# Block order at the end of an input projection, and scheduling priority for norms and last additions, in a hybrid encoder layer

## The chip, the cores and the metric

The kernel runs on one core of one Trainium2 chip. The metric is the device time of one execution in microseconds (us); lower is better. The engines are named as in the profile: PE (TensorE: matmuls, and PEld its weight loads), DVE (VectorE), ACT (ScalarE), POOL (GpSimd) and SP (SyncE, which here only issues DMA transfers; ACT issues some too).

## The reference

One encoder layer is applied to two groups of requests that share the weights: a prompt of 512 tokens and a sample of 1024, 1024 channels each. Shift, scale and gate come from a small product of each group's condition vector `c`. Cut to what matters:

```python
mod = (jax.nn.silu(c) @ w_ada + b_ada).reshape(b, N_MOD, 1, D_MODEL)
shift_a, scale_a, gate_a = mod[:, 0], mod[:, 1], mod[:, 2]
shift_m, scale_m, gate_m = mod[:, 3], mod[:, 4], mod[:, 5]

h = _rmsnorm(x, g_pre_mix) * (1.0 + scale_a) + shift_a
proj = h @ w_in                       # q 512 | k 128 | v 128 | u 512 columns
q = _apply_rope(_rmsnorm(q, g_q), cos, sin)
k = _apply_rope(_rmsnorm(k, g_k), cos, sin)
a = _attention(q, k, v)               # 8 query heads on 2 kv heads, bidirectional
p = _multiscale_pool(u, w_pool, pool_scale)
mix = jnp.concatenate([a, p], axis=-1) @ w_out
x = x + gate_a * _rmsnorm(mix, g_post_mix)

h = _rmsnorm(x, g_pre_mlp) * (1.0 + scale_m) + shift_m
f = jnp.square(jax.nn.relu(h @ w_ff1)) @ w_ff2
x = x + gate_m * _rmsnorm(f, g_post_mlp)
```

## The kernel before

Activations lie transposed, with channels on the 128 partitions and tokens along the free dimension, in stretches of 512 tokens: the prompt is one (c = 0, hf = 0), the sample two (c = 1, hf = 0 and 1). Most products are made from operands split into a rounded part and a remainder, three matmuls for each pair of 128x128 weights and 512 tokens (`block`, L156; `prod`, L869); ACT writes the rounded part, DVE the remainder (L139/L140, L881/L882, L743/L744).

The program is written as Python generators that `weave` (L25) interleaves: for each step of a foreground generator, a background generator is advanced by its rate. This fixes the order in which instructions are traced. A planner then orders them on each engine: each instruction has a priority, by default its place in the traced order, and whenever an engine is free in the planner's own model of time, the ready instruction with the earliest priority is issued next. The order so found is fixed in the program, and each engine works through its own in order. `tc.high_priority(n)` gives the instructions traced inside it the priority of a place n instructions earlier.

The order of the stages and the names that matter:

- `in_proj_p` (L488): the prompt's projection, L537 and L555.
- `in_proj_s` (L567): the sample's projection. The ten output blocks of 128 columns are taken in the order `S_IN` (L565): blocks 0 to 3 are queries, 4 keys, 5 values, 6 to 9 the pooling group's `u`. Each block has two stretches of tokens. The weights are loaded in the same order (`w_seq`). After its matmuls (L159 to L161) a query or key block is copied out of PSUM (`evac`, L377) and queued in `pend` for `qk_post` (L386): transposes on PE (`natural`, L383), squares, a sum (L395) and `rsqrt_small` (L165), the scaling and rotation on DVE (L400 to L410), transposes back, a split (L414, L415) and stores to `q_d`. `qk_post` is advanced one step at each step of the blocks that follow; what is left when the last block is done follows behind it. A pooling block is only copied and stored to `u_d` (L584); `u_post` takes it from there much later, beside the prompt's feed-forward.
- Woven into `in_proj_s` (L1302): `attention(0, ...)`, the prompt's attention (L591), at rate 1.2, and `gemv_cols` (L258) at rate 0.38: 24 of the modulation's products with `w_ada`, each a load of 512 KB on SP and one DVE instruction of 128x1024 elements (L236).
- Then `out_prep(0, 0)` (L719) loads and splits the output projection's operands, the pooled channels (k = 4 to 7) first, `out_proj(0, 0)` (L748) multiplies, with the sample's attention at rate 0.5 beside it, and `out_post(0, 0)` (L760) does the norm behind it, the gate, the residual and the next norm, with attention at rate 1.4.
- `ffn` (L825) is the prompt's feed-forward. The sample's output projection follows, and its feed-forward in a form with seven products for eight (`ff1_s`, L941; `ff2_s`, L1094).
- A norm over channels: `norm_vec` (L204) sums the squares over partitions by matmuls with one column of ones (`square_sums`, L194); `norm_sums` (L177) takes the reciprocal root of the means (ACT L170, L171; DVE L172 to L175), spreads it over the partitions by matmuls (L186) and copies the result (L191). `out_post` and `finish` call it.
- The last loop of `ff2_s` (L1213 to L1223) adds what is left of the second product to the accumulators in three parts: the first stretch of 512 tokens, then twice 256. For each of 8 blocks of channels: 12 matmuls, DVE's addition from PSUM (L1222), and `sumsq_last` (L813): ACT's square (L214), DVE's running sum (L216), and for the parts of 256 ACT's scaling by the gate (L821).
- `finish` (L1225), advanced one step at each step of that loop, does a part's norm, scaling (L1254 or L1245), residual (L1255 or L1246) and store (L1258). The part's last call runs behind everything else.

Of the kernel before, what the change touches and what calls it, by code (L numbers as in the profile page):

```python
# [7 lines left out]
F32 = mybir.dt.float32  # L8
# [3 lines left out]
AF = mybir.ActivationFunctionType  # L12
AL = mybir.AluOpType
# [3 lines left out]
KB = 8  # L17
NFB = 32
EPS = 1e-6

V_GPM, V_GQM, V_GPL, V_GQL, V_PS, V_B, V_C = 0, 8, 16, 24, 32, 36, 84
NV = 100
# [2 lines left out]
def weave(fg, bgs):  # L25

    credit = [0.0] * len(bgs)
    for _ in fg:
        for i, (bg, rate) in enumerate(bgs):
            credit[i] += rate  # L30
            while credit[i] >= 1.0:
                credit[i] -= 1.0
                next(bg, None)


def drain(g):
    for _ in g:
        pass


def chain(*gs):
    for g in gs:
        yield from g
# [3 lines left out]
def hymba_encoder_layer(ctx, tc, xp, xs, ns_, vec, gqk, rope, edge, ident_in, w_ada_c,  # L47
                        w_in_k, w_in, w_pool, w_out, w_ff1, w_ff2, yp, ys):
    nc = tc.nc
# [21 lines left out]
    st_p = ctx.enter_context(tc.tile_pool(name="stats", bufs=2))  # L71
    dram = ctx.enter_context(tc.tile_pool(name="dram", bufs=1, space=bass.MemoryType.DRAM))
    ps_mm = ctx.enter_context(tc.tile_pool(name="ps_mm", bufs=2, space=PSUM))
    ps_m = ctx.enter_context(tc.tile_pool(name="ps_m", bufs=1, space=PSUM))
# [24 lines left out]
    ident = const.tile([128, 128], F32, name="ident")  # L99
# [4 lines left out]
    eps_t = const.tile([128, 1], F32, name="eps_t")  # L104
    nc.vector.memset(eps_t, EPS)
    mod = const.tile([128, 48, 2], F32, name="mod")
# [40 lines left out]
    def next_w():  # L147

        while w_seq and len(w_ready) < AHEAD + 1:
            w_ready.append(load_w(*w_seq.pop(0)))  # L150
        return w_ready.pop(0)

    def mm_tile():
        return ps_mm.tile([128, 512], F32, tag="mm", name="mm")
# [10 lines left out]
    def rsqrt_small(out, m, n, shape, tag):  # L165

        ms = st_p.tile(shape, F32, tag=tag + "ms", name=tag + "ms")
        t = st_p.tile(shape, F32, tag=tag + "t", name="rs_t")
        u = st_p.tile(shape, F32, tag=tag + "u", name="rs_u")
        nc.scalar.activation(out=u, in_=m, func=AF.Ln, bias=eps_t, scale=1.0 / n)  # L170
        nc.scalar.activation(out=u, in_=u, func=AF.Exp, scale=-0.5)  # L171
        nc.vector.tensor_scalar(ms, m, 1.0 / n, EPS, op0=AL.mult, op1=AL.add)  # L172
        nc.vector.tensor_tensor(t, u, u, AL.mult)  # L173
        nc.vector.scalar_tensor_tensor(t, t, -0.5, ms, op0=AL.mult, op1=AL.mult)  # L174
        nc.vector.scalar_tensor_tensor(out, t, 1.5, u, op0=AL.add, op1=AL.mult)  # L175

    def norm_sums(m, keep=False):  # L177

        n = m.shape[1]
        rs = st_p.tile([128, n], F32, tag="nv_rs", name="nv_rs")
        rsqrt_small(rs, m, 1024.0, [128, n], "nv_")
        r = ps_m.tile([128, n * 128], F32, tag="m", name="nv_r")
        for j in range(n):
            nc.tensor.matmul(r[:, j * 128:(j + 1) * 128], lhsT=rs[:, j:j + 1].to_broadcast([128, 128]),  # L186
                             rhs=ident, start=True, stop=True)
        if keep:
            return r
        rt = st_p.tile([128, n * 128], F32, tag="nv_R", name="nv_R")  # L190
        nc.scalar.activation(out=rt, in_=r, func=AF.Copy)  # L191
        return rt

    def square_sums(m, sq, first, last):  # L194

        n = m.shape[1]
        for j in range(n):
            nc.tensor.matmul(m[:, j:j + 1], lhsT=sq[:, j * 128:(j + 1) * 128], rhs=ones[:, 0:1],  # L198
                             start=first and j == 0, stop=last and j == n - 1)

    def sums_tile(n=4):
        return ps_m.tile([128, 512], F32, tag="m", name="nv_m")[:, 0:n]

    def norm_vec(sqs, keep=False):  # L204

        m = sums_tile(sqs[0].shape[1] // 128)
        for i, sq in enumerate(sqs):
            square_sums(m, sq, i == 0, i == len(sqs) - 1)
        return norm_sums(m, keep)

    def sumsq_add(ss, src, m, eng):
# [350 lines left out]
            posts.append(qk_post(0, 0, xs_[b], b))  # L562
        rest.append(rp)

    S_IN = (4, 5, 9, 0, 8, 1, 7, 2, 6, 3)  # L565

    def in_proj_s():  # L567
        pend = []
        ws = {}
        for blk, hf in [(b, f) for f in range(2) for b in S_IN[:3]] + [(b, f) for b in S_IN[3:] for f in range(2)]:  # L570
            if hf == 0:
                ws[blk] = next_w()
            wh, wl = ws[blk]
            ps = mm_tile()
            for _ in block(ps, wh, wl, [h_t[1, hf, k] for k in range(KB)]):
                if pend and next(pend[0], 1) == 1:
                    pend.pop(0)
                yield
            if blk < 5:
                pend.append(qk_post(1, hf, evac(ps), blk))  # L580
            elif blk == 5:
                pend.append(v_post(1, hf, evac(ps)))
            else:
                put(u_d[blk - 6, :, hf * 512:(hf + 1) * 512], evac(ps))  # L584
        while pend:
            if next(pend[0], 1) == 1:
                pend.pop(0)
            yield
# [224 lines left out]
    def sumsq_last(c, hf, m, t0, n, fin):  # L813

        a = acc[c, hf][m][:, t0:t0 + n]
        if m == 0 and t0 == 0:
            ss_t[c, hf] = st_p.tile([128, 512], F32, tag="ss", name="ssf")
        ss = ss_t[c, hf][:, t0:t0 + n]
        sq = sumsq_add(ss, a, m, nc.vector)
        if n < 512:  # L820
            nc.scalar.activation(out=a, in_=a, func=AF.Copy, scale=gg_mlp[:, m, c:c + 1])  # L821
        if m == KB - 1:
            fin((c, hf, [ss, sq], t0, n))
# [270 lines left out]
    def ff2_s(pools):  # L1094
# [87 lines left out]
        for g, p, j in steps:  # L1182
# [15 lines left out]
            ps = chain_[j] if chained else mm_tile()  # L1198
# [14 lines left out]
        for hf, t0, n in ((0, 0, 512), (1, 0, 256), (1, 256, 256)):  # L1213
            for m in range(KB):
                if hf == 0 and 3 <= m + 2 < KB:
                    load_k(m + 2, pools["kp"])
                b = banks % 6
                banks += 1
                ps = (mm_tile() if b < 2 else ps_g.tile([128, 512], F32, tag=f"a{b - 2}", name="pb"))[:, :n]
                yield from prod(ps, wk[m], [tuple(x[:, t0:t0 + n] for x in fo["last", hf, k][0]) for k in range(4)])  # L1220
                a = acc[1, hf][m][:, t0:t0 + n]
                nc.vector.tensor_tensor(a, a, ps, AL.add)  # L1222
                sumsq_last(1, hf, m, t0, n, pools["fin"])  # L1223

    def finish(c, hf, sqs, t0=0, n=512, lands=4):  # L1225

# [55 lines left out]
    hs0, hs1 = hs[8:14] + hs[0:2], hs[2:8] + hs[14:16]  # L1282
    w_seq += [(w_in[b],) for b in S_IN]
    w_seq += [(w_out[m],) for m in range(KB)]
# [13 lines left out]
    bg = attention(0, att0)  # L1298
    gv = gemv_cols(0, cb0, 16, 40, inp)
    gv = chain([0] * 5, gv)  # L1300
    bg = chain([0] * 6, bg)
    weave(in_proj_s(), [(bg, 1.2), (gv, 0.38)])  # L1302
    drain(bg)
    drain(gv)
    att0_close()
# [17 lines left out]
    bg = attention(1, att1)  # L1323
# [17 lines left out]
    gv = gemv_rest()  # L1341
    fin = []
# [48 lines left out]
    pools = {}  # L1391
# [19 lines left out]
    fin = []  # L1411

    def close_w():
        for z in (wrb_close, wrx_close):
# [7 lines left out]
                 fin=lambda a: fin.append(finish(*a, lands=8)))  # L1422
# [79 lines left out]
```

## Time and profile before

| | us |
|---|---|
| median of 3 runs | 1666.7 (1665.64 to 1670.02) |
| the profiled execution | 1668.83 |
| its span, from the first to the last instruction | 1665.7 |
| DVE busy in it | 1213.7 |
| ACT busy in it | 854.8 |
| POOL busy in it | 10.4 |

The profiled execution is one more execution of the same program. The profile's timelines give for a row the start and the duration in us from the start of the span, the engine, the line, the operation, the tiles written and read, the shapes and a count of merged instructions; in brackets stands the idle time of the engine before it and what ended it. A row of several instructions is as long as all of them. The tile names in the rows are the program's: `nat` is a transposed block, `oh` and `ol` the parts of the output projection's operands, `q` in the last stage an accumulator, `x` a loaded residual, `ssf` the running sum of squares, `nv_m` and `nv_r` the norm's sums and its spread result.

### The profile page before, as it was taken

To read this page: it belongs to the slowest core of one execution; us is meant where nothing else is said; L and a number is where in the kernel's file an instruction comes from. 1 tells how busy PE (TensorE), PEld (TensorE's weight loads), DVE (VectorE), ACT (ScalarE), POOL (GpSimd) and SP (SyncE) were. 2 spreads that over 40 slices of the span, in tenths; PEclk is the share of its full clock that TensorE was granted. 3 is DMA by queue.
4 is the path that set the end of the run, shared out by engine and by line. 5 is a ranking of instruction groups with operands and counts; after the bars stand their busy time and mean duration, and the time that the engine had idled before them with its cause. 6 is when DMAs were issued, how large, how long until landed. Compare 5 with 4: busy or idle time off the path is not lost. (4 is left out here: it accounts for less than half of the span.)

```text
span 1665.7 us, 21550 instructions
## 1 busy us (share of the span) xinstructions
PE 1611.2 (97%) x7680; PEld 1299.9 (78%) x7680; DVE 1213.7 (73%) x1938; ACT 854.8 (51%) x1450; POOL 10.4 (1%) x27
## 2 busy tenths in 40 slices
PE   7999998999999999999999999899999999999996
PEld 4467886788888878888888888788888788888886
DVE  7898988568667675655667487878875576878757
ACT  2446664556645545546453475744445564444433
POOL 0000000000000000000000000000000000000002
PEclk8999999989999999999999999999999999999998
DMA  7756776443555553332368537566663745444334
GB/s 294 279 156 186 224 221 183 146 153 123 166 174 180 165 179 102 100 108 89 99 206 245 178 127 246 195 224 226 225 216 121 237 160 186 140 141 152 93 110 152
DMA packets 150618, 287.57 MB, mean 173 GB/s; under 512 B 15152, under 2 KB 56432, under 8 KB 150512
## 3 DMA queue, kind: packets, MB, share of 16 engines
q1 hardware_dynamic: 125824, 258.31, 47.9%
q10 hardware_dynamic: 24688, 27.89, 5.4%
q8 instruction: 60, 0.98, 0.2%
q14 instruction: 46, 0.38, 0.1%
HBM read 223.20 MB, written 61.37 MB: 171 GB/s over the span
## 5 line engine op out<-in xcount | busy, mean ns | idle before, releaser
L140 DVE TENSOR_TENSOR wl<-raw,wh 128x1024 fp32r<-128x1024 f32 (+2 forms) x106 | 121.1, 1142 | 70.4 <-ACT wh L139 69.9
L139 ACT ACTIVATE wh<-raw 128x1024 fp32r<-128x1024 f32 (+2 forms) x106 | 105.4, 995 | 120.4 <-PE mm L160 91.7
L630 ACT ACTIVATE p<-s,amx 128x1024 f32<-128x1024 f32 (+1 forms) x96 | 93.3, 972 | 108.6 <-DVE amx L628 106.7
L657 DVE TENSOR_TENSOR pl<-pT,ph 128x512 fp32r<-128x512 f32 x160 | 108.6, 686 | 54.8 <-ACT ph L656 54.3
L875 PE MATMUL pa<-fo,wh 128*128 128x512 f32 x448 | 140.4, 395 | 2.7 <-ACT x L1012 2.7
L628 DVE TENSOR_REDUCE amx<-s 128x1 f32<-128x1024 f32 (+1 forms) x96 | 100.1, 1042 | 43.5 <-PE s L618 43.1
L656 ACT ACTIVATE ph<-pT 128x512 fp32r<-128x512 f32 x160 | 93.4, 594 | 46.1 <-PE pT L653 36.8
L159 PE MATMUL mm<-hA,wh 128*128 128x512 f32 x256 | 106.7, 417 | 0.0
L159 PE MATMUL mm<-fh,wh 128*128 128x512 f32 x256 | 106.5, 417 | 0.0
L875 PE MATMUL mm<-fo,wh 128*128 128x512 f32 x336 | 104.8, 393 | 0.0
L875 PEld LDWEIGHTS pa<-fo,wh 128*128 128x128 f32 x448 | 84.8, 189 | 21.9 <-ACT x L1012 3.1
L161 PE MATMUL mm<-fh,wl 128*128 128x512 f32 x256 | 101.3, 396 | 0.0
L160 PE MATMUL mm<-fl,wh 128*128 128x512 f32 x256 | 101.0, 394 | 0.0
L160 PE MATMUL mm<-hA,wh 128*128 128x512 f32 x256 | 100.9, 395 | 0.0
L161 PE MATMUL mm<-hA,wl 128*128 128x512 f32 x256 | 100.5, 394 | 0.0
L653 PE MATMUL pT<-ident,p 128*128 128x128 f32 x640 | 96.6, 275 | 1.4 <-DVE pl L657 0.9
L618 PE MATMUL s<-kst,q 128*128 128x512 f32 x320 | 93.9, 406 | 4.0 <-ACT p L630 2.0
L653 PEld LDWEIGHTS pT<-ident,p 128*128 128x128 f32 x640 | 79.3, 142 | 22.6 <-issue 2.4
L875 PE MATMUL pa<-fo,wl 128*128 128x512 f32 x224 | 88.1, 393 | 0.0
L881 ACT ACTIVATE fo<-raw 128x512 fp32r<-128x512 f32 x106 | 66.3, 631 | 38.3 <-DMA raw<-f_d 31.5
L882 DVE TENSOR_TENSOR fo<-raw,fo 128x512 fp32r<-128x512 f32 x106 | 71.2, 689 | 15.8 <-ACT fo L881 15.2
L666 PE MATMUL x<-ph,vst 128*128 128x256 f32 x320 | 81.7, 285 | 0.5 <-ACT ph L656 0.5
(291 smaller groups left out, 3922.5 us busy)
## 6 DMA issues: line engine op xcount, KB each, us to landing
raw<-in_w_ff SPq DMA_DIRECT2D x56, 512.0 KB, 3.8
f_d<-x SPq DMA_DIRECT2D x98, 256.0 KB, 2.8
raw<-f_d SPq DMA_DIRECT2D x98, 256.0 KB, 3.0
raw<-in_w_ada_c SPq DMA_DIRECT2D x40, 512.0 KB, 3.9
g<-in_w_ada_c SPq DMA_DIRECT2D x24, 512.0 KB, 4.3
q<-q_d SPq DMA_DIRECT2D x96, 128.0 KB, 3.6
raw<-in_w_out SPq DMA_DIRECT2D x24, 512.0 KB, 3.8
rawx<-in_w_ff SPq DMA_DIRECT2D x20, 512.0 KB, 4.0
```

The source lines that it names most:

```text
L139: nc.scalar.activation(out=fh, in_=r[:, :n], func=AF.Copy)
L140: nc.vector.tensor_tensor(fl, r[:, :n], fh.bitcast(F32), AL.subtract)
L159: nc.tensor.matmul(ps, lhsT=wh[:, k, :], rhs=ah, start=(i == 0), stop=False)
L160: nc.tensor.matmul(ps, lhsT=wh[:, k, :], rhs=al, start=False, stop=False)
L161: nc.tensor.matmul(ps, lhsT=wl[:, k, :], rhs=ah, start=False, stop=(i == len(ks) - 1))
L618: nc.tensor.matmul(s[:, f * 512:(f + 1) * 512], lhsT=q[:, h, p, :], rhs=kst[c][:, kv, f * 512:(f + 1) * 512].bitcast(F32R), start=(p == 0) ...
L628: nc.vector.tensor_reduce(mx, s[:, :n], AX.X, AL.max, negate=True)
L630: nc.scalar.activation(out=pr, in_=s[:, :n], func=AF.Exp, bias=mx, accum_out=den)
L653: nc.tensor.transpose(t[:, k, :], pr[:, (4 * f + k) * 128:(4 * f + k + 1) * 128], ident)
L656: nc.scalar.activation(out=hi, in_=t, func=AF.Copy)
L657: nc.vector.tensor_tensor(lo, t, hi.bitcast(F32), AL.subtract)
L875: nc.tensor.matmul(ps, lhsT=x[:, k, :], rhs=y, start=start and k == i == 0, stop=k == n - 1 and i == 2, skip_group_check=not start)
```

## The change

Three things change. In `S_IN` blocks 7 and 2 change places, and 6 and 3, so that the projection ends with block 6 and not with block 3; the products of `w_ada` woven into it get rate 0.5 in place of 0.38. The norm's sums in `norm_vec` and the whole chain in `norm_sums` are traced with a priority 300 instructions earlier. The same holds for the addition and `sumsq_last` in the last loop of `ff2_s`. The sums of squares that `out_post` itself writes for the prompt's second norm keep their priority. What is computed stays the same.

```diff
+URGENT = 300

     def norm_sums(m, keep=False):
         n = m.shape[1]
-        rs = st_p.tile([128, n], F32, tag="nv_rs", name="nv_rs")
-        rsqrt_small(rs, m, 1024.0, [128, n], "nv_")
-        r = ps_m.tile([128, n * 128], F32, tag="m", name="nv_r")
-        for j in range(n):
-            nc.tensor.matmul(r[:, j * 128:(j + 1) * 128], lhsT=rs[:, j:j + 1].to_broadcast([128, 128]),
-                             rhs=ident, start=True, stop=True)
-        if keep:
-            return r
-        rt = st_p.tile([128, n * 128], F32, tag="nv_R", name="nv_R")
-        nc.scalar.activation(out=rt, in_=r, func=AF.Copy)
-        return rt
+        with tc.high_priority(URGENT):
+            rs = st_p.tile([128, n], F32, tag="nv_rs", name="nv_rs")
+            rsqrt_small(rs, m, 1024.0, [128, n], "nv_")
+            r = ps_m.tile([128, n * 128], F32, tag="m", name="nv_r")
+            for j in range(n):
+                nc.tensor.matmul(r[:, j * 128:(j + 1) * 128], lhsT=rs[:, j:j + 1].to_broadcast([128, 128]),
+                                 rhs=ident, start=True, stop=True)
+            if keep:
+                return r
+            rt = st_p.tile([128, n * 128], F32, tag="nv_R", name="nv_R")
+            nc.scalar.activation(out=rt, in_=r, func=AF.Copy)
+            return rt

     def norm_vec(sqs, keep=False):
-        m = sums_tile(sqs[0].shape[1] // 128)
-        for i, sq in enumerate(sqs):
-            square_sums(m, sq, i == 0, i == len(sqs) - 1)
+        with tc.high_priority(URGENT):
+            m = sums_tile(sqs[0].shape[1] // 128)
+            for i, sq in enumerate(sqs):
+                square_sums(m, sq, i == 0, i == len(sqs) - 1)
         return norm_sums(m, keep)

-    S_IN = (4, 5, 9, 0, 8, 1, 7, 2, 6, 3)
+    S_IN = (4, 5, 9, 0, 8, 1, 2, 7, 3, 6)

                 a = acc[1, hf][m][:, t0:t0 + n]
-                nc.vector.tensor_tensor(a, a, ps, AL.add)
-                sumsq_last(1, hf, m, t0, n, pools["fin"])
+                with tc.high_priority(URGENT):
+                    nc.vector.tensor_tensor(a, a, ps, AL.add)
+                    sumsq_last(1, hf, m, t0, n, pools["fin"])

-    weave(in_proj_s(), [(bg, 1.2), (gv, 0.38)])
+    weave(in_proj_s(), [(bg, 1.2), (gv, 0.5)])
```

## The prediction, made before the changed kernel ran

> **What bounds the kernel now.** I read the page first, then the list of PE's waits, then the timeline of each engine around the longest of them. The page says how much there is to win at all:
>
> ```profile
> PE 1611.2 (97%) x7680; PEld 1299.9 (78%) x7680; DVE 1213.7 (73%) x1938; ACT 854.8 (51%) x1450; POOL 10.4 (1%) x27
> ```
>
> PE is busy for 1611.2 of 1665.7 us. The change takes no matmul away, so it can win only PE's idle time, 54.5 us, and the time in which PE runs at a reduced clock. Both lie in few places. The first is the end of the input projection (PE's timeline):
>
> ```profile
> 273.91 0.40 PE L161 MATMUL mm<-hh,wl 128*128 128x512 f32 x1
> 275.86 0.66 PE L383 MATMUL nat<-ident,xT 128*128 128x128 f32 x4 [1.55 <-ACT xT L377]
> 276.38 0.74 PE L159 MATMUL mm<-oh,wh 128*128 128x512 f32 x2
> 281.90 1.08 PE L383 MATMUL nat<-ident,y 128*128 128x128 f32 x4 [4.79 <-DVE rs_t L173]
> 282.64 0.78 PE L160 MATMUL mm<-ol,wh 128*128 128x512 f32 x1
> ...
> 301.02 1.16 PE L618 MATMUL s<-kst,q 128*128 128x512 f32 x4 [1.79 <-DMA q<-q_d]
> ```
>
> The last projection matmul ends at 274.31. Then PE, which works in order, reaches the transposes (L383) of the last query block: it waits 1.55 us for the copy out of PSUM, does two matmuls of the output projection, and waits 4.79 us for the normed and rotated block. DVE shows what it waits for:
>
> ```profile
> 277.83 1.21 DVE L236 CUSTOM_DVE_ANT_0 g<-g,cb 128x1024 f32<-128x1024 f32 x1
> ...
> 281.07 0.68 DVE L410 TENSOR_TENSOR y<-y,t 128x512 f32<-128x512 f32 x1
> ...
> 281.75 0.68 DVE L744 TENSOR_TENSOR ol<-accA,oh 128x512 fp32r<-128x512 f32 x1
> ```
>
> The last instruction of the rotation (L410) ends at 281.75, and only behind it does DVE write `ol`, which the output projection needs. A modulation product (L236) of 1.21 us stands in the same stretch. The idle time has an after-effect, seen when stretches are cut at the clock's steps (columns: length, busy time of PE, PEld, DVE, ACT, POOL, then the granted clock, DMA share, GB/s):
>
> ```profile
> 175.00:200.00 25.00, 25.00 (x134) 20.13 (x134) 23.36 (x54) 16.49 (x37) 0.00 (x0) 1.00 0.68 205
> 200.00:225.00 25.00, 24.78 (x137) 20.45 (x136) 23.21 (x50) 15.65 (x35) 0.00 (x0) 1.00 0.76 231
> 225.00:250.00 25.00, 24.98 (x136) 20.52 (x135) 21.14 (x47) 15.18 (x33) 0.00 (x0) 1.00 0.73 235
> 279.84:286.67 6.83, 4.77 (x14) 3.93 (x15) 6.83 (x17) 1.52 (x4) 0.00 (x0) 0.50 0.14 29
> 358.35:372.00 13.65, 13.65 (x59) 12.66 (x59) 8.28 (x13) 6.29 (x11) 0.00 (x0) 0.50 0.52 188
> 1327.73:1331.14 3.41, 2.98 (x7) 2.40 (x8) 2.92 (x4) 2.02 (x4) 0.00 (x0) 0.50 0.99 300
> ```
>
> In 279.84 to 286.67 the granted clock is 0.50: the 4.77 us of PE work there would have taken half as long, so another 2.4 us are lost. The place costs 1.55 + 4.79 + 1.79 + 2.4 = **10.5 us**.
>
> The second place is the end (DVE's, PE's and ACT's timelines):
>
> ```profile
> 1646.31 2.48 DVE L1245 TENSOR_TENSOR q<-q,nv_r 128x512 f32<-128x512 f32 x4
> 1648.70 2.21 DVE L1246 TENSOR_TENSOR x<-q,x 128x512 f32<-128x512 f32 x2
> 1650.83 1.07 DVE L1222 TENSOR_TENSOR q<-q,pb 128x256 f32<-128x256 f32 x3
> 1651.83 0.94 DVE L216 TENSOR_TENSOR ssf<-ssf,sq 128x256 f32<-128x256 f32 x2
> ```
> ```profile
> 1646.03 3.57 PE L875 MATMUL pb<-fo,wk 128*128 128x256 f32 x28
> 1652.91 0.98 PE L198 MATMUL nv_m<-ones,ssf 128*128 128x1 f32 x4 [3.31 <-DVE ssf L216]
> 1653.76 0.99 PE L198 MATMUL nv_m<-ones,sq 128*128 128x1 f32 x4
> ```
> ```profile
> 1652.72 0.40 ACT L214 ACTIVATE sq<-q 128x256 f32<-128x256 f32 x1
> 1653.16 0.51 ACT L821 ACTIVATE q<-q,gg_mlp 128x256 f32<-128x256 f32 x1
> 1654.79 0.26 ACT L170 ACTIVATE rs_u<-nv_m,eps_t 128x2 f32<-128x2 f32 x1 [1.12 <-PE nv_m L198]
> ```
>
> The last product ends at 1649.60. Three additions (L1222) that PE's results have been ready for wait until 1650.83, because DVE first does the previous part's scaling and residual (L1245, L1246). From PE's end to the start of the last norm (L170) pass 5.19 us; everything behind is a serial chain to the last output.
>
> **Part 1: the block order and the faster modulation.** Block 3, a query block, gives the last place to block 6, a pooling block, which after its matmuls needs only a copy and a store. Block 3's two posts (the copy, two sets of transposes, the rotation, two stores each) then lie beside 48 matmuls of block 6 and no longer behind the projection. No instruction is added or removed; the order of the weight loads follows S_IN, and stores to u_d, read much later, merely change places on ACT's queue. So the 1.55 and 4.79 us go, and with them the reduced clock.
>
> The rate 0.5 for 0.38 draws the 24 products together:
>
> ```profile
> L236 DVE CUSTOM_DVE_ANT_0 g<-g,cb x24: 1201/1216/1226, 156.4 to 277.8; 128x1024 f32<-128x1024 f32 x24
> ```
>
> They stand (277.8 - 156.4) / 23 = 5.3 us apart; at the new rate 5.3 x 0.38 / 0.5 = 4.0 us. The last then comes about 23 x 1.3 = 30 us earlier, near 248, and the end of the projection is free of them. Their loads move with them on SP's queue, ahead of query and weight loads behind which they stood. The price is DVE in the middle: in 25 us there are 6.2 products instead of 4.7, 1.5 x 1.3 = 1.9 us more, where the rows leave it 1.64 and 1.79 us of idle time.
>
> What is late next? The output projection's own first operands. ACT's rows give 0.57 us for `oh`, DVE's row above 0.68 for `ol`:
>
> ```profile
> 275.22 0.58 ACT L377 ACTIVATE xT<-mm 128x512 f32<-128x512 f32 x1
> 275.70 1.14 ACT L743 ACTIVATE oh<-accA 128x512 fp32r<-128x512 f32 x2
> ```
>
> If they can be made only once the projection's tiles are free, PE waits 0.57 + 0.68 and two handovers, 1.5 us; if not, nothing. I take 1.5, since `oh` came only after 274.31 here too. The wait for `q` at 301.02 is for a load that is issued late because its buffer is freed late; with the posts gone it is issued earlier, but I don't see how early the planner puts the matmul: between 0 and 1.79, I take 0.9. For DVE's crowding I take 1.1, between 0 and 3.8 (1.9 us in each of two stretches). Sum: 10.5 - 1.5 - 0.9 - 1.1 = **7.0 us** won; at best 10.5, at worst 10.5 - 1.5 - 1.79 - 3.8 - 1.7 = 1.7.
>
> The last term, 1.7 us, is for the clock, from this row:
>
> ```profile
> 1328.16 1.22 PE L875 MATMUL pa<-fo,wh 128*128 128x512 f32 x2 [2.68 <-ACT x L1012]
> ```
>
> An idle time of 2.68 us was followed by 3.41 us at clock 0.50 (the last row of the stretches), which costs half of that. The Trainium skill, "TensorE: Matmul & The Clock Gate", section "HAM oscillation — how this bites in real kernels", asks for no idle gap above about 3.4 us. By that rule the remaining 1.5 us would never cost clock and the worst case would be 3.4; the trace does not agree, since 2.68 us were enough here.
>
> **Part 2: the additions.** With the higher priority L1222 and the squares behind it go ahead of L1245 and L1246 as soon as a bank is complete. After 1649.60 there remain one addition (1.07 / 3 = 0.36), its square (0.40), the last sums (0.99) and handovers (0.25): 2.0 us, and up to 1.1 more if DVE has just begun an L1246 (2.21 / 2). That is 2.0 to 3.1 instead of 5.19. I take a win of **2.5 us**. The displaced L1245 and L1246, 4.7 us, are not lost: DVE has nothing else to do while the last chain runs on PE and ACT. If that cover were gone, the last scaling would start up to 1.1 us late.
>
> **Part 3: the norms' chains.** The code runs eleven with sums of PE, and two more for the sample's first norm. In most of them PE has matmuls of another stage, so a shorter chain is worth nothing; where that cover is missing is the norm after the prompt's output projection, where PE has only attention:
>
> ```profile
> 348.04 0.16 DVE L173 TENSOR_TENSOR rs_t<-rs_u 128x4 f32<-128x4 f32 x1 [0.20 <-ACT rs_u L171]
> 348.12 1.22 DVE L628 TENSOR_REDUCE amx<-s 128x1 f32<-128x1024 f32 x1
> 349.25 0.15 DVE L174 SCALAR_TENSOR_TENSOR rs_t<-rs_t,nv_ms 128x4 f32<-128x4 f32 x1
> 349.32 0.68 DVE L657 TENSOR_TENSOR pl<-pT,ph 128x512 fp32r<-128x512 f32 x1
> 349.92 0.15 DVE L175 SCALAR_TENSOR_TENSOR nv_rs<-rs_t,rs_u 128x4 f32<-128x4 f32 x1
> ```
>
> A maximum and a subtraction of attention stand between the chain's instructions: 349.25 - 348.20 = 1.05 and 349.92 - 349.40 = 0.52 us, 1.6 in all. They move behind the chain, and attention is later by as much, beside matmuls that fill PE. I take **1.0 us**, between -1 (attention late) and 3.2 (twice 1.6, for the stage's second norm).
>
> **Sum.** 7.0 + 2.5 + 1.0 = 10.5 us. The profiled execution took 1668.83 us (span 1665.7), which gives 1658.3; the median of the runs is 1666.7, 2.1 less, which gives 1656.2. I predict 1656.2.
>
> **The rivals.** *Crowded DVE.* In 175 to 225 DVE has 3.4 us left, and the products want 3.8. If the posts and the prompt's attention fall behind by several us, the output projection waits for attention instead of for the post. Part 1 then wins about 1.7: 1666.7 - 1.7 - 2.5 = 1662.5. Against it: DVE's idle time before the end, and five products fewer there.
>
> *Full clock after the first output projection.* The 13.65 us at 0.50 cost 6.8 us. If shorter chains keep PE denser there, they come on top: 1656.2 - 6.8 = 1649.4. Against it: the sums' matmuls themselves, one column wide, fill much of that stretch.
>
> *The priority doesn't bite.* The planner orders each engine by readiness in its own model of time; if it believes L1222's input to be late, L1245 still goes first. Parts 2 and 3 win nothing: 1659.7.
>
> *Slower: PE's order.* An urgent matmul is put into PE's order where the model has its input ready; where DVE is later on the chip, everything behind it stands. The row for that:
>
> ```profile
> 1028.54 1.02 PE L198 MATMUL nv_m<-ones,ss 128*128 128x1 f32 x8 [0.78 <-DVE ss L216]
> ```
>
> 0.78 us here at the earlier priority. With two sums and one broadcast in eleven chains, 33 places: it eats the 10.5 us from 0.32 us a place on. At 0.78 each the cost is 25.7, the result 1666.7 - 10.5 + 25.7 = 1681.9; half of that gives 1669. For it speaks only that one row; against it that PE shows no wait at most of these matmuls.
>
> **How the numbers follow.** Forecast 0.56, with its own range 1651 to 1661; crowded DVE 0.14; full clock 0.12; no bite 0.12; PE's order 0.06. Within 0.3%, 5.0 us, a measurement of this kernel can't be told from no change: faster means below 1661.7, slower above 1671.7. Faster: 0.54 of the forecast, 0.12 of full clock, 0.10 of no bite, 0.02 of crowded DVE, 0.78. Slower: 0.04. The same: 0.18. For 8 in 10 the range takes in the crowded case above and most of the full clock's below: 1648 to 1665.
>
> **What would show it.** Right: between the last L161 of the projection and the second matmul of the output projection PE idles under 2.5 us, with no stretch at clock 0.50 behind; the last L236 stands before 260; L170 follows PE's last product within 3.2 us; no L628 or L657 stands inside L173 to L175. Wrong: PE waits for `ol` or `oh` of the attention heads, or for L383, for more than 3 us near 280; L1245 still ahead of L1222; new idle time before L198 or L186 elsewhere.

## The result, and the profile after

Five executions of each kernel, one beside the other on one chip: 1683.3 us (1676.89 to 1687.11) with the change, 1668.54 us (1665.64 to 1670.02) without it. The ratio is 1.0083 with an interval of [1.0059, 1.0108]: the changed kernel is **slower by 0.8%**, some 14 us, where 10.5 us less were predicted. In the changed kernel the lines behind the new `URGENT` have moved: up to 175 by one, the norm's broadcast from 186 to 188, its sums from 198 to 200, the lines of the posts, the attention and the output projection by three, those of the last additions by four.

The page's first part, for the profiled execution (span 1681.0 us, before 1665.7):

```profile
PE 1624.0 (97%) x7680; PEld 1310.0 (78%) x7680; DVE 1213.9 (72%) x1938; ACT 856.0 (51%) x1450; POOL 10.6 (1%) x27
```

The same 7680 matmuls keep PE busy for 1624.0 us in place of 1611.2. Of the 15.3 us that the span has grown, 12.8 are matmuls that take longer, and only 2.5 are idle time (1681.0 - 1624.0 = 57.0 against 54.5). In this profile the loss is mostly one of **clock**. Where it sits is seen when PE's first and last matmuls of each stage are set against each other:

| stage, by PE's matmuls, us | before | after | difference |
|---|---|---|---|
| start to the last matmul of the input projection | 274.31 | 267.45 | -6.9 |
| from there to the first of the prompt's output projection | 2.07 | 26.64 | +24.6 |
| the prompt's output projection | 65.85 | 59.69 | -6.2 |
| its post stage, to the first matmul of the feed-forward | 36.39 | 39.99 | +3.6 |
| from there to the last product of all | 1270.99 | 1273.68 | +2.7 |
| from there to the end | 16.10 | 13.59 | -2.5 |

The end is shorter by what was predicted. The projection ends 7 us earlier, and in the 26.6 us that follow PE is busy for only 12.9, most of them at half the clock. PE's timeline there:

```profile
267.06 0.39 PE L162 MATMUL mm<-hh,wl 128*128 128x512 f32 x1
268.24 0.73 PE L621 MATMUL s<-kst,q 128*128 128x512 f32 x2 [0.79 <-ACT p L633]
...
271.17 0.85 PE L656 MATMUL pT<-ident,p 128*128 128x128 f32 x4 [2.06 <-ACT p L637]
...
284.36 1.08 PE L386 MATMUL nat<-ident,y 128*128 128x128 f32 x4 [5.33 <-DVE y L413]
285.24 1.06 PE L656 MATMUL pT<-ident,p 128*128 128x128 f32 x4
...
294.09 0.79 PE L160 MATMUL mm<-oh,wh 128*128 128x512 f32 x1 [3.67 <-ACT oh L746]
```

Behind the projection stand the last units of the prompt's attention (`s`, `pT`) and the transposes of block 3's posts (`nat`), which the prediction had put beside block 6. For 5.33 us PE waits at a `nat` for the rotation, and the attention's `pT`, ready before, stands behind it in PE's order. The output projection then waits for `oh`. ACT's timeline shows why that comes so late:

```profile
267.40 0.69 ACT L633 ACTIVATE p<-s,amx 128x512 f32<-128x512 f32 x1 [3.09 <-DMA q<-q_d]
...
285.48 0.60 ACT L417 ACTIVATE rh<-nat 128x512 fp32r<-128x512 f32 x1 [4.58 <-PE nat L386]
...
289.60 0.38 ACT L674 ACTIVATE ao<-x 128x256 f32<-128x256 f32 x1 [2.68 <-PE x L670]
290.46 0.60 ACT L417 ACTIVATE rh<-nat 128x512 fp32r<-128x512 f32 x1 [0.47 <-PE nat L386]
290.46 0.38 ACTq L675 DMA_DIRECT2D a_d<-ao  x1
291.81 1.25 ACTq L422 DMA_DIRECT2D q_d<-rh  x2
293.40 2.19 ACT L746 ACTIVATE oh<-accA 128x512 fp32r<-128x512 f32 x4 [2.35 <-issue]
```

`oh` stands behind the attention's last copy (`ao`, 289.60), the last post's copy (`rh`, 290.46) and its stores (291.81). Before, it stood ahead of both last posts. ACT's timeline of the kernel before, where `oh` came at 275.70:

```profile
283.02 0.60 ACT L414 ACTIVATE rh<-nat 128x512 fp32r<-128x512 f32 x1 [1.67 <-PE nat L383]
...
290.29 0.60 ACT L414 ACTIVATE rh<-nat 128x512 fp32r<-128x512 f32 x1 [6.67 <-PE nat L383]
```

The last post is copied at 290.29 before and at 290.46 after: the work beside the matmuls ends at the same moment in both. Before, its last part lay beside the output projection; now that waits for all of it. Two stretches at half the clock lie in this gap, a third stands later, in the post stage (columns as in the prediction):

```profile
271.57:274.98 3.41, 3.41 (x16) 2.95 (x14) 1.83 (x4) 1.68 (x5) 0.00 (x0) 0.51 0.24 87
281.73:298.80 17.07, 9.94 (x30) 7.59 (x31) 11.85 (x23) 5.93 (x11) 0.00 (x0) 0.50 0.43 117
370.48:390.96 20.48, 20.48 (x95) 19.99 (x95) 12.28 (x21) 8.43 (x16) 0.00 (x0) 0.50 0.42 142
```

The first two are new or longer (before, 6.83 us in all); the third was 13.65 us long, and another 3.41 us are new ahead of it, from 360.24.

The end, on PE, ACT and DVE:

```profile
1663.50 3.93 PE L878 MATMUL pb<-fo,wk 128*128 128x256 f32 x31
1669.39 0.58 PE L200 MATMUL nv_m<-ones,ssf 128*128 128x1 f32 x4 [1.96 <-DVE q L1249]
```
```profile
1670.45 0.26 ACT L171 ACTIVATE rs_u<-nv_m,eps_t 128x2 f32<-128x2 f32 x1 [1.41 <-PE nv_m L200]
```
```profile
1667.64 0.41 DVE L1226 TENSOR_TENSOR q<-q,pb 128x256 f32<-128x256 f32 x1
1667.97 0.68 DVE L1250 TENSOR_TENSOR x<-q,x 128x512 f32<-128x512 f32 x1
1668.57 0.67 DVE L1249 TENSOR_TENSOR q<-q,nv_r 128x512 f32<-128x512 f32 x1
```

The addition now follows 0.21 us behind the last product (1667.43), and the norm begins 3.02 us behind it in place of 5.19.

### The profile page after: what moved, and what is told of

Its sections match the earlier page's. It is cut to its first block, busy times and chain, and to the rows that moved or that the text cites. A ratio compares the mean times of both kernels' runs of the same rounds, so it can differ in the third digit from the quotient of the medians.

```text
span 1681.0 us, 21539 instructions
## 1 busy us (share of the span) xinstructions
PE 1624.0 (97%) x7680; PEld 1310.0 (78%) x7680; DVE 1213.9 (72%) x1938; ACT 856.0 (51%) x1450; POOL 10.6 (1%) x27
## 4 chain that ended last, share of the span: by engine, by line
PE 79%; DMA 10%; DVE 7%; ACT 2%; issue 2%; SPq 1%; DVEq 0%; ACTq 0%
PE pa L878 19%; PE mm L160 9%; PE mm L161 9%; PE mm L162 9%; PE mm L878 9%; DMA raw<-in_w_ada_c 5%; PE pc L878 5%; PE s L621 3%; PE pT L656 3%; PE nv_m L200 2%; PE x L670 2%; PE x L669 2%; PE pb L878 1%; DVE raw L239 1%; DMA raw<-in_w_ff 1%
## 5 line engine op out<-in xcount | busy, mean ns | idle before, releaser
L660 DVE TENSOR_TENSOR pl<-pT,ph 128x512 fp32r<-128x512 f32 x160 | 108.8, 686 | 60.2 <-ACT ph L659 60.0
L631 DVE TENSOR_REDUCE amx<-s 128x1 f32<-128x1024 f32 (+1 forms) x96 | 100.0, 1041 | 41.1 <-PE s L621 40.7
L670 PE MATMUL x<-pl,vst 128*128 128x256 f32 x320 | 83.4, 291 | 0.5 <-DVE pl L660 0.3
```

Source lines behind the costliest of these rows:

```text
L631: nc.vector.tensor_reduce(mx, s[:, :n], AX.X, AL.max, negate=True)
L660: nc.vector.tensor_tensor(lo, t, hi.bitcast(F32), AL.subtract)
L670: nc.tensor.matmul(x, lhsT=v, rhs=st["pl"][:, k], start=False, stop=(k == nkb - 1))
```

## The experiments

Each is an edit of the kernel before unless it says otherwise. Ratios are against the kernel before on the same chip; the time in us is the ratio's, at 1670. Two theories stood at first for the projection, **R** (the higher rate crowds DVE) and **O** (the order itself), and **N** for the norms' priority.

**1 to 4: the parts of the change alone and in pairs.** Order alone, rate alone, both priorities without them, and order with rate:

```diff
e1  -S_IN = (4, 5, 9, 0, 8, 1, 7, 2, 6, 3)    +S_IN = (4, 5, 9, 0, 8, 1, 2, 7, 3, 6)
e2  -[(bg, 1.2), (gv, 0.38)]                  +[(bg, 1.2), (gv, 0.5)]
e3  the changed kernel with S_IN and the rate of before
e4  e1 and e2
```

> Only the order of the blocks is changed (block 6 last), against the kernel before. Theory R (the rate is to blame: the faster products crowd DVE, so that the posts and the prompt's attention fall behind): without the rate this order behaves as was forecast, the stretch from the last projection matmul to the first output-projection matmul stays under 6 us, and the time is 5 to 9 us below the kernel before. Theory O (the order is to blame: with a pooling block last the projection's matmuls run ahead, and attention's last units and the last post are left with nothing beside them): that stretch is 15 to 27 us here too, and the time is 5 to 12 us above.

> Only the rate of the modulation's products is changed (0.5 for 0.38). Theory R: attention falls behind, the projection's last matmul comes earlier than at 274.3 and the gap behind it grows from 2 us to over 10; the time is 5 to 12 us above the kernel before. Theory O: nothing is late at the end, DVE is freer there, the 4.79 us wait shrinks; the time is 0 to 4 us below.

> Both priorities are changed, the order and the rate are those of before. If the loss lies in the projection alone (theories R and O): the projection's end is as before (last matmul near 274, output projection from 276), the tail behind the last product is 2 to 3 us shorter, and the time is 1 to 4 us below. Theory N (the norms' priority in the sample's first norm or the prompt's second shifts the stages behind it): the stretch from the output projection's end to the first feed-forward matmul grows from 36.4 to 39 us or more, as in the changed kernel (40.0), and the time is the same or above.

> Order and rate are changed, the priorities are not: the changed kernel without parts 2 and 3. If the parts add up, this is the changed kernel less the tail's gain: the gap behind the projection 20 to 27 us, the stretch between output projection and feed-forward 36.4 us, and the time 8 to 14 us above the kernel before. If the gap comes only with the norms' priority (theory N, through the sample's first norm), the gap is under 6 us and the time below.

| kernel | ratio, interval | us | attention's last copy | projection's last matmul | gap behind it | output projection's last matmul |
|---|---|---|---|---|---|---|
| before | | | 271.2 | 274.3 | 2.1 | 342.2 |
| e1 order | 1.0018 [1.0003, 1.0032] | +3.0 | 283.0 | 273.3 | 16.0 | 347.0 |
| e2 rate | 1.0015 [0.9998, 1.0032] | +2.5 | 277.9 | 269.3 | 10.6 | 344.5 |
| e4 order and rate | 1.0059 [1.0038, 1.0081] | +9.9 | 289.0 | 265.7 | 27.8 | 351.7 |
| after | 1.0083 [1.0059, 1.0108] | +13.9 | 289.6 | 267.5 | 26.6 | 353.8 |
| e3 priorities | 1.0039 [1.0024, 1.0054] | +6.5 | 271.2 | 274.2 | 2.5 | 342.8 |

Neither R nor O is the cause alone. The attention's last copy is the last start in these rows (the line of `ao`, one row from each of before, e1, e2, e4 and after):

```profile
L671 ACT ACTIVATE ao<-x x16: 363/386/398, 150.9 to 271.2; 128x256 f32<-128x256 f32 x16
```
```profile
L671 ACT ACTIVATE ao<-x x16: 367/386/395, 151.3 to 283.0; 128x256 f32<-128x256 f32 x16
```
```profile
L671 ACT ACTIVATE ao<-x x16: 364/386/394, 151.0 to 277.9; 128x256 f32<-128x256 f32 x16
```
```profile
L671 ACT ACTIVATE ao<-x x16: 380/384/396, 149.5 to 289.0; 128x256 f32<-128x256 f32 x16
```
```profile
L674 ACT ACTIVATE ao<-x x16: 373/384/393, 150.4 to 289.6; 128x256 f32<-128x256 f32 x16
```

The order delays it by 11.8 us, the rate by 6.7; together that is 18.5, and e4 shows 17.8, the changed kernel 18.4. **The delays of the attention add up.** The times may not (3.0 and 2.5 alone, 9.9 together), but the 4.4 us between sum and pair are within what the three intervals allow. In each row the earlier end of the projection and the shorter output projection together give back more than half of what the gap has grown by; the output projection ends 4.8, 2.3 and 9.5 us later. In e3 attention and gap are as before: the norms have no part in it, and their price lies elsewhere.

**5: is it the attention's end?** New order and rate, and the attention woven in faster (theory G), against rival D, that DVE's work decides, whoever has it first:

```diff
 (with the new S_IN)
-weave(in_proj_s(), [(bg, 1.2), (gv, 0.38)])
+weave(in_proj_s(), [(bg, 1.6), (gv, 0.5)])
```

> New order and new rate, and the prompt's attention woven at 1.6 instead of 1.2 steps. Theory G (the output projection cannot start before the attention's last unit is stored and its operands stand behind the last units and posts in ScalarE's order, so the attention's end is what the gap of 27.8 us waits for): attention's last copy at 268 to 276 us instead of 289, the gap 8 to 16 us, 5 to 12 us faster than the kernel with order and rate alone. Rival D (VectorE's work up to that point decides, whoever gets it first): what the attention wins the posts lose, and the start of the output projection or its first stretch moves by under 3 us.

The time falls to 1.0002 [0.9987, 1.0017], 9.5 us under e4. The row of `ao` and the output projection's first row on PE:

```profile
L671 ACT ACTIVATE ao<-x x16: 373/384/412, 150.1 to 265.2; 128x256 f32<-128x256 f32 x16
```
```profile
278.28 0.74 PE L159 MATMUL mm<-oh,wh 128*128 128x512 f32 x2 [1.30 <-ACT oh L743]
```

The attention ends 24 us earlier than in e4 and the gap is 1.3 us. G holds. But the projection's matmuls end at 277.0, and the output projection at 342.2, where it ended in the kernel before: with all in its place the new order wins nothing.

**6 and 7: is it DVE's load?** New order and rate with DVE relieved, by GpSimd, or by halving the products (e11 leaves out the second half of each product's columns, so its output is not the layer's; it measures and is no kernel to use):

```diff
e10 +                if jb % 2:
    +                    nc.gpsimd.tensor_tensor(r, r, cb, AL.mult)
    +                    nc.scalar.activation(out=r, in_=r, func=AF.Copy, accum_out=mod[:, jb, c:c + 1])
    +                else:
                         tc.keep_in_program_order(gemv_part(c, jb, r, cb, r))
e11 -                tc.keep_in_program_order(gemv_part(c, jb, r, cb, r))
    +                tc.keep_in_program_order(gemv_part(c, jb, r[:, :512], cb[:, :512], r[:, :512]))
```

> New order and new rate, and every second product of the modulation (12 of 24, 1.2 us of VectorE each) made by GpSimd with ScalarE's sum. Theory D (VectorE's load decides when the attention and the posts end): 12 x 1.3 = 15.6 us less VectorE work ahead of the gap; attention's last copy 8 to 15 us earlier than 289 us, gap 12 to 20 instead of 27.8 us, 6 to 12 us faster than the kernel with order and rate alone. Rival (in-order waits on ScalarE and TensorE set it, not the load): gap over 24 us, time within 3 us of that kernel.

> New order and new rate, and each of the 24 modulation products woven into the projection is made over the first half of its columns only, so the modulation from column 16 on is not the reference's. Takes 24 x about 0.6 = 14 us from VectorE ahead of the gap and leaves the rest of the program as it is. Theory D (VectorE's load decides when the prompt's attention and the posts end): attention's last copy 8 to 14 us earlier than in the kernel with order and rate alone, where the gap was 27.8 us; gap 10 to 20 us, output projection over 7 to 13 us earlier, 6 to 12 us faster in all. Rival Q (the attention's place in the weave and the in-order waits decide, not the load): gap over 23 us, time within 3 us of that kernel.

e10 missed altogether: 1.0157 [1.0132, 1.0182], 26 us slower than the kernel before, the projection's last matmul at 295.2. It took nothing from DVE. One product on POOL, and DVE's row beside it:

```profile
185.77 2.35 POOL L270 TENSOR_TENSOR g<-g,cb 128x1024 f32<-128x1024 f32 x1 [6.84 <-DMA g<-in_w_ada_c]
```
```profile
185.83 2.57 DVE L640 TENSOR_SCALAR p<-p,aden 128x512 f32<-128x512 f32 x1
```

This scaling has a median of 0.486 us in the kernel before; here it takes 2.57 us and ends where POOL's product has ended. DVE's busy time is 1215.5 us with 12 products fewer. So e10 says nothing on D. e11 does: 0.9988 [0.9970, 1.0006], 12 us under e4, with 12.9 us less on DVE (busy for 1200.9 us, in e4 for 1213.8):

```profile
L671 ACT ACTIVATE ao<-x x16: 375/386/393, 150.2 to 277.1; 128x256 f32<-128x256 f32 x16
```
```profile
282.31 0.79 PE L159 MATMUL mm<-oh,wh 128*128 128x512 f32 x1 [4.11 <-ACT oh L743]
```

The attention ends 12 us earlier than in e4, the gap is 4.8 us, and the output projection ends at 341.6, 10 us earlier than in e4. Both are true, then: the attention's end sets the gap, and DVE's load, or the attention's share of DVE, sets the attention's end. Rival Q falls.

**8 to 11: where do the norms lose?** All norms alone; then without the priority in the prompt's post stage; then in the sample's post stages alone; then outside the post stages alone:

```diff
e6  the priority in norm_vec and norm_sums, nothing else of the change
e12 +with tc.high_priority(pr):      pr = URGENT, but 0 in out_post(0, 0)
e14 +with tc.high_priority(pr) if pr else nullcontext():      pr = URGENT in out_post(1, ...) alone
e15 the same, pr = URGENT in all but out_post
```

> Kernel before with the norms' priority alone. Theory N (it costs in the two stages behind the prompt's output projection, where the kernel with both priorities was 2.3 and 3.5 us longer, and the last additions' part gives back 2.5 there): 7 to 9 us slower, with about 20 us at a granted clock of 0.50 behind the prompt's output projection, and an end as long as before. Rival: the loss of the kernel with both priorities came from their sum: then 3 us slower or less.

> The norms' priority alone, but not in the post stage of the prompt's output projection. Theory N1 (the loss of 7 us sits in that stage, where attention's work that filled PE is used up early and PE is left with one-column matmuls at half the clock): the stage is 36 to 37 us again, with at most 14 us at half the clock, and the whole is within 2.5 us of the kernel before. Rival N2 (the loss is spread over the later stages, in half-clock stretches of their own): the stage is back and 4 to 5 us of the loss remain.

> The norms' priority in the sample's post stages alone, everything else as before. Theory S (the second half's post stage, where in the last run the first broadcast came 6 us sooner, but the additions behind it waited for their inputs' DMAs, VectorE had put the weights' splits off, and PE stood 2.5 us and fell to half the clock for 7 to 10 us): nearly the whole loss, 4 to 7 us slower; first broadcast 4 us behind the last output-projection matmul instead of 9.6, PE's wait for the second norm about 2.5 instead of 0.4 to 0.8 us. Rival T (the loss is in the norms outside the post stages): within 1.5 us of before.

> The norms' priority outside the post stages alone (the two inputs' norms and the final ones). Theory S: within 1.5 us of before. Rival T: 4 to 7 us slower, to be seen at the start of the program or in the last part, whose last matmul was 0.6 us later with the priority.

| kernel | ratio, interval | us | prompt's post stage | end of the sample's output projection to the next stage's first product (`pc`) |
|---|---|---|---|---|
| before | | | 36.4 | 79.5 |
| e6 | 1.0041 [1.0021, 1.0061] | +6.8 | 38.7 | 83.9 |
| e12 | 1.0040 [1.0024, 1.0057] | +6.7 | 36.4 | 83.3 |
| e14 | 1.0017 [1.0002, 1.0033] | +2.8 | 36.5 | 84.5 |
| e15 | 0.9995 [0.9983, 1.0008] | -0.8 | 36.5 | 79.5 |

The norms' price as a whole is clear, 6.8 us by e6, and e15 has none of it. Where it is paid inside the post stages is less clear: these two stages are compared by one profile each, and what such a profile is worth is said at each. In the prompt's post stage the chain itself is no shorter; DVE's timeline of the changed kernel:

```profile
359.92 0.15 DVE L174 TENSOR_TENSOR rs_t<-rs_u 128x4 f32<-128x4 f32 x1
359.99 0.68 DVE L660 TENSOR_TENSOR pl<-pT,ph 128x512 fp32r<-128x512 f32 x1
360.59 0.15 DVE L175 SCALAR_TENSOR_TENSOR rs_t<-rs_t,nv_ms 128x4 f32<-128x4 f32 x1
360.66 0.68 DVE L660 TENSOR_TENSOR pl<-pT,ph 128x512 fp32r<-128x512 f32 x1
361.26 0.15 DVE L176 SCALAR_TENSOR_TENSOR nv_rs<-rs_t,rs_u 128x4 f32<-128x4 f32 x1
```

Subtractions of the attention (L660) still stand between its steps, as each step waits for the one before and other work fits between; `nv_rs` is done 7.6 us behind the output projection (353.78), before 7.8. What moved is PE's order behind it. PE's timeline of e6, then its window at half the clock:

```profile
354.28 4.33 PE L200 MATMUL nv_m<-ones,x 128*128 128x1 f32 x24 [0.82 <-ACT x L780]
```
```profile
355.36:375.84 20.48, 20.48 (x94) 19.99 (x94) 12.28 (x21) 8.32 (x16) 0.00 (x0) 0.50 0.46 143
```

The stage is at half the clock for 20.48 us, before for 13.65, although PE is busy all the time; in e12 and e14, with no higher priority there, the stage is back at 36.4 and 36.5 us. That the new order is the reason is **not shown**. The 24 one-column matmuls in a row are no news (before, 32 follow one another from 355.14 on). And e8 has PE's matmuls of this stage in the very order of the kernel before, and yet this window:

```profile
357.86:378.34 20.48, 20.48 (x91) 19.37 (x91) 12.12 (x20) 9.12 (x18) 0.00 (x0) 0.50 0.44 145
```

Its stage is 39.0 us long. The twelve other profiles in this document that keep that order have 35.7 to 37.8 us, the three with the new one (after, e3, e6) 40.0, 38.7 and 38.7. So the 2.3 us are likely, but one profile in thirteen shows them without the priority.

The other place is the post stage of the sample's second half. PE's timeline of e14 there, where the output projection ends at 1002.69, and the kernel before's first broadcast, where it ended at 1000.68 (its sums behind are in the prediction, at 1028.54):

```profile
1006.37 1.13 PE L189 MATMUL nv_r<-ident,nv_rs 128*128 128x128 f32 x8
1030.06 1.02 PE L201 MATMUL nv_m<-ones,ss 128*128 128x1 f32 x8 [2.81 <-DVE ss L220]
```
```profile
1010.29 1.13 PE L186 MATMUL nv_r<-ident,nv_rs 128*128 128x128 f32 x8
```

The first broadcast comes 3.7 us behind the output projection in place of 9.6: here the priority shortens what it was meant to shorten. But the second norm's sums start 27.4 us behind it, before 27.9, so of 5.9 us only 0.5 are left at the stage's other end. DVE's timeline of e14 between them shows the new wait:

```profile
1014.29 0.69 DVE L779 TENSOR_TENSOR accA<-accA,x 128x512 f32<-128x512 f32 x1 [1.69 <-DMA x<-in_xs]
...
1024.27 0.69 DVE L779 TENSOR_TENSOR accA<-accA,x 128x512 f32<-128x512 f32 x1 [0.93 <-DMA x<-in_xs]
...
1027.41 0.69 DVE L779 TENSOR_TENSOR accA<-accA,x 128x512 f32<-128x512 f32 x1 [0.58 <-DMA x<-in_xs]
```

The residual additions were started earlier and now wait for their inputs (before, one of them waits, for 0.67 us). PE, which before waited 0.78 us for the sums, waits 2.81, and runs at half the clock behind that for 6.82 us, before for 3.41. But e11, without any norm's priority, has the same length behind a wait of 0.90 us (PE's timeline, then the window):

```profile
1031.90:1038.72 6.82, 6.82 (x24) 6.05 (x25) 2.50 (x6) 3.35 (x8) 0.00 (x0) 0.50 0.33 105
```
```profile
1027.50 1.02 PE L198 MATMUL nv_m<-ones,ss 128*128 128x1 f32 x8 [0.90 <-DVE ss L216]
```
```profile
1029.25:1036.08 6.83, 6.83 (x26) 6.06 (x25) 2.50 (x6) 2.83 (x6) 0.00 (x0) 0.50 0.51 173
```

So the longer wait is shown, and the clock behind it is not shown to be its doing. The last column of the table is weak evidence too: the twelve profiles that keep PE's order of this stage have 77.5 to 83.1 us there, the five with the new order (after, e3, e6, e12, e14) 80.6 to 84.5.

By the medians e14 lost 2.8 us, where 4 to 7 were expected. e14 and e15 together with the 2.3 us of the prompt's stage make 4.3 of e6's 6.8 us; the rest is within the intervals. e12 does not fit: it lost 6.7 us although the prompt's stage was back, where some 2 were to be expected from e14 and e15. Its priority of 0 is not the same as none (the order of PE, DVE and ACT differs from the kernel before's); that this is the reason was not tried, and stays **open**.

**12 to 14: what pays?** The last additions' priority alone, twice, and together with the new order, the new rate and the faster attention:

```diff
e5, e16  the priority in the last loop of ff2_s, nothing else of the change
e13      the same, with S_IN of e1 and [(bg, 1.6), (gv, 0.5)]
```

> Kernel before with the third part alone: only the last additions and their squares get the priority. Theory L (the last additions' priority shortens the end by what the changed kernel showed there, 5.45 instead of 7.61 us from the last product to the end of the last broadcast): 2.0 to 3.0 us faster, and no stage ahead of the last part moves by over 0.5 us. Rival: the gain at the end hangs on the norms' priority as well (the last chain is one of them): then 0 to 0.7 us.

> The kernel before with the priority on the last additions and their squares alone, a second time and in more rounds. Theory L: ratio 0.9985 to 0.9992 with an interval under 1, and 5.8 instead of 7.6 us from the last product to the end of the last broadcast. Rival: the end is shorter, but what else the priority moves gives it back: ratio 0.9995 to 1.0005.

> New order, new rate, the prompt's attention woven at 1.6, and the last additions' priority, without the norms' priority. By the sum of the runs so far (the kernel with the faster attention was 0.4 us from the kernel before, the additions alone 1.9 us faster): 0.5 to 3 us faster than the kernel before, with a gap behind the projection under 3 us and the end 2 us shorter. If the additions' gain was chance: within 0.5 us or slower.

e5 has 0.9989 [0.9972, 1.0007], e16 0.9989 [0.9975, 1.0004]: 1.8 us, and each interval just holds no change. In both profiles the time from the last product to the end of the last broadcast is shorter, 5.77 and 5.76 us for 7.61. So the gain is likely, not proved. e13 missed: 1.0007 [0.9990, 1.0023], though its gap is 1.3 us and its end 5.78. No kernel was found that beats the kernel before beyond its interval.

**15: the kernel before again,** for the spread of one program:

> The kernel before again, unchanged, for a second profile. If the stretches at half the clock belong to the program, they stand where the first profile has them (13.65 us behind the prompt's output projection, 3.41 us near 1031) and the span is within 1 us of 1665.7. If they fall by chance as well, one or two stretches of 3.41 us more or fewer appear, each for about 1.7 us of the span, up to some 1672 us.

One execution, 1664.41 us, span 1662.6. Two of its stretches at half the clock:

```profile
355.20:362.00 6.80, 6.80 (x29) 6.31 (x30) 6.36 (x11) 3.82 (x8) 0.00 (x0) 0.50 0.84 292
...
597.60:601.00 3.40, 3.28 (x11) 2.27 (x10) 3.00 (x6) 0.40 (x1) 0.00 (x0) 0.50 0.21 33
```

The post stage has two stretches of 6.83 us with full clock between them, in place of one of 13.65; the one near 1031 is gone, one at 597.6 is new. Differences of 1 to 3 us between single profiles of two kernels can therefore not be read as the kernels'; the medians carry them.

## Why the prediction was wrong

**Part 1, order and rate: -7.0 forecast, +9.9 measured (e4).** The steps that held: the projection's last product L236, now L239, stands at 257.0 (under 260 was forecast), and no instruction is added. The step that failed is **"what is late next?"**. It named the output projection's own first operands, for 1.5 us, and the crowding of DVE, for 1.1. What is late next is the **prompt's attention**: the step assumed that work moved away from the end of the projection lies beside block 6's 48 matmuls. PE went through these 48 matmuls ahead of it. The posts' last copy did not move (290.29, 290.46), the attention's end moved by 18.4 us, and the output projection, which before began at 276.4, behind the attention's end (271.2) and beside the last post, now waits for both. The crowding was priced by the DVE time lacking in 25 us (1.9 us, twice). That was the wrong quantity: the whole products that come earlier all delay the same chain (halved in e11, they delay its end by 12 us less). On the attention's last copy the rate's term is 6.7 us by e2, and the order's 11.8 by e1. That in e1 it is the posts of blocks 2 and 3, one turn earlier on DVE, that delay the chain is inferred from this and not shown by a run of its own.

"So the 1.55 and 4.79 us go": PE's wait of 4.79 us at L383 came back as 5.33 us at the same line (now L386), 2.5 us later.

The rival "crowded DVE" had this mechanism, the output projection waiting for attention instead of for the post. Its price was wrong: it let part 1 still win 1.7 us. It also left out the clock: the attention's chain is alone on PE, and 15.8 of the 26.6 us run at half the clock (271.57 to 274.98, and from 281.73 to 294.09).

**Part 2, the additions: -2.5 forecast, -2.5 measured** between the last product and the end in the changed kernel, -1.8 by e5 and e16. The norm begins 3.02 us behind the product, inside the 2.0 to 3.1. It is at the upper end, and by the trace PE's sums wait there for L1249 (1668.57), a scaling of the previous part, not for the square.

**Part 3, the norms: -1.0 forecast (from -3.2 to +1), +6.8 measured (e6).** Its first step failed: L628 and L657 (now L631 and L660) did not move behind the chain; two L660 still stand in it. Its other step failed as well, "in most of them a shorter chain is worth nothing", so that nothing else was priced. Where the chain's first part did become shorter, by 5.9 us, additions ran into their inputs and PE into a wait of 2.81 us (e14). How the 6.8 us are divided between the stages stays open. With part 1's 9.9 and the additions' -1.8 they make 14.9 us, and the changed kernel lost 13.9.

**The rival on the other side** held PE's order responsible: idle time in front of urgent matmuls, 0.32 us a place. It had the row of the right place, 1028.54, and of its 33 places that one did grow, from 0.78 to 2.81 us in e14. In sum it did not: PE's waits at the norms' sums and broadcasts are 11.4 us after (4.2, 2.5, 2.0, 1.9 and 0.8 in the list of PE's waits) and 11.5 before (4.0, 3.3, 2.5, 0.9, 0.8). The loss came from the attention's end, 9.9 us, and from the norms' priority in the post stages. Of the other rivals, "full clock" had a real lever, but no run moved it in its direction (13.65 us became 20.48, which e8 shows without the priority as well), and "the priority doesn't bite" fell: L1226 goes ahead of L1249 and L1250.

The last term of the worst case, 1.7 us, took a wait of 2.68 us as enough for a stretch at half the clock. It is not always: at the same place 2.49 us in b0 come with 3.41 us at 0.50, and 3.29 us in e13 with none.

**The range and chances** failed by the same step as part 1: with the attention's delay worked out, a part 1 that loses would have been a case of its own; 0.04 was left for slower.

## What to carry to other kernels

Before the last place of a stage is given to work with a shorter tail, look at what the next stage waits for, and follow that chain back: if it is fed by another engine that is already full, PE's matmuls are only filler, and ending them earlier uncovers the chain. Where one engine is nearly full, a weave's rates are shares of it: here raising one put off the other's end, and the one that the next stage waits for has to come first. A higher priority shortens a chain only where its next step is ready, and what it starts earlier then waits for its own inputs; so look for the next wait, and for what PE has left to do meanwhile. And before a stage's length in one profile is read as a kernel's, look at how much it differs among kernels that leave the stage alone.

## What the hardware showed

**Half the clock with PE busy throughout.** From 355.36 to 375.84 in e6 PE is busy for all of 20.48 us, with one-column matmuls and transposes among its 94, at a granted clock of 0.50; in e8 it is the same from 357.86 to 378.34. All stretches are multiples of 3.41 us, and the second profile of one program has them elsewhere. The Trainium skill, "TensorE: Matmul & The Clock Gate", section "What's actually happening", tells of a free-running window of 3413 ns; these lengths and their shifting agree with it. The rule of the Trainium skill's same page on idle gaps, which the prediction weighed (section "HAM oscillation — how this bites in real kernels", none above about 3.4 us), does not keep the clock up here: a wait of 2.49 us in b0 came with 3.41 us at 0.50. Nor does the length alone decide, since 3.29 us at the same place in e13 came with a full clock.

**GpSimd holds up VectorE.** The scaling with a median of 0.486 us took 2.57 us beside one product on POOL. The Trainium skill, "SBUF — State Buffer", section "Who interferes with whom", has an exclusive lock on a pair of ports that the two engines share; e10's rows agree, and a product taken off DVE in this way cost more than it saved.

**A store's issue holds up ACT.** In the changed kernel two stores of `q_d` occupied ACT's queue for 2.34 us from 265.01. The attention's exponential behind them had its last input, DVE's maximum, at 265.58 and began at 267.40, 0.05 us behind the second store: 1.8 of the 3.09 us of idle time in its row. The row names a load as what ended the wait; the times speak for the stores.
